# A hybrid RWKV-7, S5 and conv-FFN layer on one core: larger bursts in the level step, GELUs put behind its last copies, squares on GpSimd, and six residuals added through PSUM at the end

## The chip, the cores and the metric

The kernel runs on one core of a Trainium2 chip. The time is device microseconds (us) of one execution of the whole program, from its first to its last instruction and what the runtime puts around it; the table below gives the median of three runs, and one further execution was recorded by the hardware profiler. Engines are named as the profile names them: PE is TensorE (PEld its weight loads), DVE is VectorE, ACT is ScalarE, POOL is GpSimd, SP is SyncE, which here only issues DMAs.

## The reference

One layer over x of 1 x 1024 x 1024 floats (SEQ 1024, D_MODEL 1024), all in float32:

```python
h = rms_norm(x, norm_mix_pre)
proj = h @ w_in                                # [RWKV r,k,v + low-rank downs | S5 input | two gates]
gates = sigmoid(proj[..., N_RWKV_COLS + S5_WIDTH:] + b_gate)
g_rwkv, g_s5 = split(gates, 2)
o_rwkv = rwkv7_branch(proj[..., :N_RWKV_COLS], ...) @ w_branch_rwkv     # 8 heads of 64, delta-rule state
o_s5 = s5_branch(u_s5, ...) @ w_branch_s5      # 32 groups of 16 channels, 64 complex states each:
                                               # y = Re(C s) + D u;  y = gelu(y);  y * sigmoid(y @ w_glu + b_glu)
mixed = (g_rwkv * o_rwkv + g_s5 * o_s5) @ w_out
x = x + rms_norm(mixed, norm_mix_post)
h = rms_norm(x, norm_ffn_pre)
z = causal depthwise conv of width 3 over h @ w_up;  gate, val = split(z)
f = (gelu(gate) * val) @ w_down                # hidden width 2816
x = x + rms_norm(f, norm_ffn_post)
```

## The kernel before

Everything is held transposed: channels on the 128 partitions, time along the free axis in two halves of 512 (called th = 0 and 1). A weight tile is loaded as wf, rounded to fp32r by ACT (wh, L160), and the rest wf - wh is taken by DVE (wl, L161); an activation is split the same way (hh by ACT at L245, hl by DVE at L246). A product of one 128x128 weight block with 512 columns is then three matmuls in a row: wh with hh, wh with hl, wl with hh (L180, L181, L182, one "step"). The order of PE's instructions is written by a small planner in the program: each part of the work is a generator that emits some instructions and yields (its cost on PE, how long its next piece should wait, a weight); lanes of such generators run by priority, and between them `background()` puts in steps from the queue of projections, so that a stated wait of 13 us means 13 us of PE work, by the planner's count, ahead of the next piece. The other four engines' orders come from a list scheduler with priorities; where the program wants a fixed order there it adds one by `add_manual_dep(..., ORDER)`, which sets an order and no semaphore. Each engine takes its instructions in its order; the DMA queues of SP, ACT and POOL are issued in those engines' orders too.

The stages, with the lines the change touches:

- `start` (to about 40 us): the first pre-norm (th = 0), the split of its eight tiles (`self.splits[k]` holds the two instructions, ACT L245 and DVE L246, of tile k), and the S5 input products (PE L1158) with weights loaded by `s5_ws`. `behind_low` is a pair of instructions behind which the following wh and wl casts are ordered.
- S5, four groups b of eight (to about 300 us): tables on DVE, then `s5_batch`: scans (DVE L643), two rotations z*sn and z*cs on DVE (L645, L646), a yield with the stated wait T_SCAN (T_SCAN0 for b = 0), and then 24 matmuls in the order toep, ca, cb (PE L651, L652, L653). L652 reads what L646 wrote.
- RWKV: four blocks i of chunks, each with fronts, a 32x32 triangular inverse on DVE and POOL, `rwkv_level`, and `rwkv_chain` over eight chunks c (PE L870, L888, L899, L901, L906, L911; ACT L874, L903, L909; DVE L902, L913). `rwkv_level` joins 32x32 inverse blocks into 64x64 ones: for each of two steps and each u of two, 16 matmuls of 32x32 into PSUM (L838, then L840), in two halves of 8 with a yield after each half, and two ACT copies out (L839, L841). What L839 writes is what L840 reads.
- The GLU of S5: its inputs come back from DRAM by a POOL DMA (L1253) and go through GELU on ACT (`s5_y`, L1254, the first of them with an ACT_TABLE_LOAD); hh and hl of them feed the GLU's steps. They are ordered behind `self.squared`, an ACT square in an RWKV front (L700).
- Post-norm (to about 895 us): for th = 1 `post_norm` makes eight tiles mx (DVE L1417, L1418), squares each on ACT (L276) and adds the squares up in a chain of seven (DVE L278); PE L264 sums the last one over the partitions, DVE takes the reciprocal root, PE L290 spreads it. Meanwhile the FFN's first up-projections for th = 0 run on PE, ACT moves them out (L1520), and POOL issues their stores to DRAM (L1521, tensors AH).
- FFN up and down to about 1503 us, and the end: for the last half, two sums of squares (sq, DVE L1729) are summed by PE (L264) into ss, DVE makes the root (rv, rsy), PE L290 spreads it to a bank, DVE L1829 scales the eight tiles, and the residual is added in one of two ways: for the tiles 4 to 7 by two matmuls with the identity into one PSUM bank, one with the residual (L1898) and one with the scaled tile (L1831), and an ACT copy out (L1832); for the tiles 0 to 3 by DVE (L1729). SP issues the eight output DMAs (L1835).

Of the kernel before, what the change touches and what calls it, by code (L numbers as in the profile page):

```python
# [14 lines left out]
ALU = mybir.AluOpType  # L15
# [58 lines left out]
class Kern:  # L74
# [195 lines left out]
    def tx(self):  # L270
        return self.nrm.tile([128, 512], F32, tag="Tx", name=self.nm("tx"), bufs=NTX)

    def square_into(self, acc, x):

        sq = self.tm()
        self.nc.scalar.activation(sq, x, AF.Square)  # L276
        if acc is not None:
            self.nc.vector.tensor_tensor(sq, sq, acc, ALU.add)  # L278
        return sq

    def rstd(self, ss, eps, scale):
# [339 lines left out]
    def s5_batch(self, b, d, ys):  # L621

        nc, V, G, A = self.nc, self.nc.vector, self.nc.gpsimd, self.nc.scalar
        s = self.s5
        mm = nc.tensor.matmul
        ca, cb, cs, sn, toep, wT = (d[n] for n in ("ca", "cb", "cs", "sn", "toep", "wT"))

        u8 = self.u8[b]
        z = self.t4(shape=(128, 8, 128))
        G.memset(z[:, :, 0:1], 0.0)  # L630
        rot = self.t4(shape=(128, 8, 128))
        yield 0, T_US
        p1, p2 = (self.chk().rearrange("p (g n) -> p g n", n=128) for _ in range(2))
        for p, o in ((p1, 0), (p2, 1)):
            for g in range(8):
                mm(p[:, g], wT[:, g, o:o + 2, :], u8[:, g, :], start=g % 4 == 0, stop=True, skip_group_check=True)
        r2 = self.t4(shape=(128, 8, 128))
        V.tensor_tensor(rot, p1, cs, ALU.mult)
        V.tensor_tensor(r2, p2, sn, ALU.mult)
        V.tensor_tensor(rot, rot, r2, ALU.add)  # L640
        for g in range(8):
            gg = b * 8 + g
            V.tensor_tensor_scan(z[:, g, 1:128], s["rho"][:, gg:gg + 1].to_broadcast([128, 127]),  # L643
                                 rot[:, g, 0:127], 0.0, ALU.mult, ALU.add)
        V.tensor_tensor(rot, z, sn, ALU.mult)  # L645
        V.tensor_tensor(z, z, cs, ALU.mult)  # L646
        y8 = self.t4(shape=(128, 8, 128))
        yield 3.6, T_SCAN if b else T_SCAN0
        ps = self.chk().rearrange("p (g n) -> p g n", n=128)
        for g in range(8):  # L650
            mm(ps[:, g], toep[:, g], u8[:, g, :], start=g % 4 == 0, stop=False, skip_group_check=True)  # L651
            mm(ps[:, g], ca[:, g, 1:9, :], z[:, g, :], start=False, stop=False, skip_group_check=True)  # L652
            mm(ps[:, g], cb[:, g, 1:9, :], rot[:, g, :], start=False, stop=True, skip_group_check=True)  # L653
        A.copy(y8, ps)
        for th in range(2):
            A.dma_start(ys[th].rearrange("c g j n -> j c g n"), y8[:, :, th * 64:th * 64 + 64])
        yield 5.4, 0
# [166 lines left out]
    def rwkv_level(self, d, spare):  # L824

        A, V = self.nc.scalar, self.nc.vector
        mm = self.nc.tensor.matmul
        gr = d["gr"]
        p0 = self.chk(1).rearrange("p (u c t) -> p u c t", u=2, t=32)
        p0, p1 = [p0[:, u] for u in range(2)], [self.chb().rearrange("p (c t) -> p c t", t=32) for u in range(2)]  # L830
        xz = (self.tg("x", 1, pool=self.rka) if spare else self.tg("ld", NLD)).rearrange("p (u c t) -> p u c t", u=2, t=32)
        top, bot = [[slice(64 * h + o, 64 * h + o + 32) for h in range(2)] for o in (0, 32)]
        t0, t1 = slice(0, 32), slice(32, 64)
        for h, sl in enumerate(top):
            self.levelled = V.transpose(xz[sl].rearrange("p u c t -> p (u c) t"), gr[sl, :, :, h, t0].rearrange("p u c t -> p (u c) t"))
        yield 0, T_LT
        kw = dict(stop=True, skip_group_check=True)
        steps = ((lambda u, c, h: mm(p1[u][bot[h], c], gr[top[h], u, c, h, t1], xz[top[h], u, c], start=c == 0, **kw),  # L838
                  lambda u, h: A.copy(xz[bot[h], u], p1[u][bot[h], 0:8])),  # L839
                 (lambda u, c, h: mm(p0[u][top[h], c], xz[bot[h], u, c], gr[bot[h], u, c, h, t1], start=c == 0, **kw),  # L840
                  lambda u, h: A.copy(gr[top[h], u, :, h, t1], p0[u][top[h], 0:8])))  # L841
        for step, evict in steps:
            for u in range(2):
                for c in range(8):
                    for h in range(2):
                        step(u, c, h)
                    if c % 4 == 3:
                        yield 0.3, 0.3, 2.0
                for h in range(2):
                    evict(u, h)  # L850
            yield 0, T_LV

    def rwkv_chain(self, d):
# [319 lines left out]
    def start(self, xp):  # L1173

        tc = self.tc

        def go(gen, n=1):
            for _ in range(n):
                with tc.high_priority(HPN if gen in norms else HPW):
                    next(gen, None)  # L1180
        with tc.high_priority(HPN):
            xs = [self.load_x(0, xp)]
            self.setup()
            norms = [self.norm(0, xs[0], xp)]
            self.idle = self.gmp()
        consts = self.s5_setup()
        with tc.high_priority(HPS):
            next(consts)
        go(norms[0], 5)
        newton = self.newton  # L1190
        self.behind_x = self.last_x

        def first(o, behind=None):
            with tc.high_priority(HPN - HPW):
                r = []
                for b in (2, 3):
                    self.behind_low = behind
                    r.append(self.load_w(self.a["w_in"][14 + b][:, o:o + 512]))
                return r
        p = first(0, (None, newton))  # L1200
        go(norms[0])
        q = first(512, (self.splits[1][0], self.splits[2][1]))
        self.behind_x, self.behind_low = None, (None, None)
        ws = [[(x[0] + y[0], x[1] + y[1]) for x, y in zip(p, q)]]
        with tc.high_priority(HPW):
            xs.append(self.load_x(1, xp))
            norms.append(self.norm(1, xs[1], xp))
        with tc.high_priority(HP):
            self.nc.sync.dma_start(self.csts[:, 128:NCST], self.a["cst"][:, 128:NCST])
            self.s5w = {}  # L1210
            self.s5_load(0)
            self.s5_load(1)
        a = self.s5_in((2, 3), 0, ws[0])
        go(a, 8)
        with tc.high_priority(HPW):
            ws.append(self.s5_ws((0, 1)))
        with tc.high_priority(HPS):
            self.setup_vecs()
            self.newton = newton
            next(consts, None)  # L1220
        go(a)
        b = self.s5_in((0, 1), 0, ws[1])
        go(b)
        for _ in range(4):
            go(norms[1])
            go(b)
        go(norms[1])
        go(b, 1)
        go(norms[1])
        go(b, 3)  # L1230
        c = self.s5_in((0, 1), 1, ws[1])
        go(c, 9)
        for b in range(2):
            self.load_u8(b)
# [164 lines left out]
    def post_norm(self, src, y, th, gain, resid, store, squares=None):  # L1399


        nc = self.nc
        o = slice(th * 512, th * 512 + 512)
        xs, sq = [], []
# [10 lines left out]
        for k in range(NK):  # L1415
            y = src[k]
            nc.vector.scalar_tensor_tensor(y, y, self.vec(gain, k), bc, ALU.mult, ALU.mult)  # L1417
            (nc.vector if k % 2 or squares is not None else nc.gpsimd).tensor_tensor(y, y, xs[k], ALU.add)  # L1418
            load(k + NTX)
            if squares is not None:  # L1420
                sq.append(self.square_into(sq[-1] if sq else None, y))
                (nc.sync if th else nc.scalar).dma_start(store(k, o), y)
            else:
                (nc.sync if th else nc.gpsimd).dma_start(store(k, o), y)
# [256 lines left out]
    def down(self, dq0, dqf, dqt, dqa, dqs, dqb):  # L1681
# [3 lines left out]
        nc, V, A = self.nc, self.nc.vector, self.nc.scalar  # L1685
# [150 lines left out]
        acc = [None, None]  # L1836
        f = [[None] * NK for _ in range(2)]
        b, x = [bank(m) for m in range(4)], [bank(4 + m) for m in range(4)]
# [47 lines left out]
        d, last = {}, []  # L1886
# [9 lines left out]
        def resid_sum(m, b):  # L1896
            sums[m] = bank(b)
            mm(sums[m], self.cst("ident"), d["xs1"][m], start=True, stop=False)  # L1898
        resid_sum(4, 0)
        resid_sum(5, 1)  # L1900
        self.sumsq(ss, last[0], True)
        self.sumsq(ss, acc[1], False)
        for m, b in ((6, 4), (7, 5)):
            resid_sum(m, b)
        y = self.rstd(ss, 1e-6, 1.0 / D)
        bc = bank(3)
        self.spread(bc, y)
        outputs(1, f[1], bc, d["xs1"], sums)

    def build(self):  # L1910
# [183 lines left out]
                yield from self.urgent(out)  # L2094


T_SCAN0 = 17.0
T_US, T_TAB0, T_TAB, T_TRIG, T_SCAN = 5.0, 26.0, 20.0, 12.0, 13.0
T_LD, T_LT = 14.0, 3.0
NEVA = 4  # L2100
# [92 lines left out]
```

## Time and profile before

| what | value |
|---|---|
| median of 3 runs | 1525.88 us (1525.83 to 1526.22) |
| the profiled execution | 1524.13 us, of which its span is 1522.3 us |
| PE busy | 1469.8 us, 97% of the span |
| DVE busy | 1158.5 us, 76% |
| ACT busy | 726.6 us, 48% |
| POOL busy | 180.2 us, 12% |
| mean granted TensorE clock | 0.991 |

A row of the timeline gives the start, the length in us, the engine, the line, the operation with its output and inputs, how many instructions were put together, and in brackets how long the engine had stood idle before them and whose instruction ended that. A row of the waits gives an engine and line, whom it waited for, and the total, the count and the longest. A table of windows gives the busy time of each engine in each stretch, and PEclk, the mean granted clock there.

### The profile page before, as it was taken

What the parts mean: (1) busy time and instruction counts of PE and PEld (TensorE: products, weight loads), DVE (VectorE), ACT (ScalarE), POOL (GpSimd) and SP (SyncE); (2) the same over time, 40 slices, a digit from 0 to 9 for tenths busy, and PEclk for the clock granted to TensorE, in tenths of its full rate; (3) what the DMA queues carried; (4) which work ended last, traced back from release to release, by engine and by line L of the source; (5) the groups of instructions that cost most, each with busy time, mean ns of one, the idle gap of its engine ahead of it and who ended that gap; (6) DMA issues with size and microseconds to landing.
All of it is one profiled execution on the core that took longest, in us unless ns stands there. A gap on an engine that the chain in (4) does not pass through costs nothing.

```text
span 1522.3 us, 23902 instructions
## 1 busy us (share of the span) xinstructions
PE 1469.8 (97%) x8804; PEld 1166.1 (77%) x8804; DVE 1158.5 (76%) x2157; ACT 726.6 (48%) x1209; POOL 180.2 (12%) x340
## 2 busy tenths in 40 slices
PE   7999999999999998999999999999999999999997
PEld 5788787787677675666788778888888887888875
DVE  7989974765655594975767888888888888698767
ACT  5465444331453434556635555555555555444451
POOL 0022111124021232030110010000000000000000
PEclk9999999999999998999999999999999999999999
DMA  6455344444332446452456575233333336944712
GB/s 211 135 154 159 98 139 145 143 135 152 107 124 96 128 120 192 146 167 70 157 189 199 182 242 180 93 108 117 113 110 117 112 109 225 333 154 138 246 59 111
DMA packets 121558, 225.26 MB, mean 148 GB/s; under 512 B 31024, under 2 KB 37168, under 8 KB 121440
## 3 DMA queue, kind: packets, MB, share of 16 engines
q1 hardware_dynamic: 90576, 154.77, 32.5%
q0 software_dynamic: 21024, 64.71, 12.9%
q10 hardware_dynamic: 9840, 4.24, 1.1%
q8 instruction: 69, 1.13, 0.3%
q14 instruction: 49, 0.40, 0.1%
HBM read 164.16 MB, written 57.41 MB: 146 GB/s over the span
## 4 chain that ended last, share of the span: by engine, by line
PE 44%; DVE 4%; DMA 4%; ACT 1%; issue 1%; SPq 0%; DVEq 0%; ACTq 0%
PE d L1779 8%; PE rp L1600 5%; PE rp L1602 5%; PE rp L1601 5%; PE mm L1602 2%; PE mm L1600 2%; PE mm L1601 2%; DMA st<-in_w_down_dram 2%; PE ch L181 1%; PE mm L180 1%; PE ch L182 1%; PE mm L181 1%; PE gm L180 1%; PE ch L180 1%; PE mm L182 1%
## 5 line engine op out<-in xcount | busy, mean ns | idle before, releaser
L180 PE MATMUL gm<-hh,wh 128*128 128x512 f32 x672 | 283.1, 421 | 1.9 <-DVE ev L1057 1.9
L181 PE MATMUL gm<-hl,wh 128*128 128x512 f32 x672 | 264.9, 394 | 0.1
L182 PE MATMUL gm<-hh,wl 128*128 128x512 f32 x672 | 264.7, 394 | 0.0
L160 ACT CAST wh<-wf 128x512 fp32r<-128x512 f32 x181 | 111.9, 619 | 171.5 <-PE gm L181 88.5
L161 DVE TENSOR_TENSOR wl<-wf,wh 128x512 fp32r<-128x512 f32 x181 | 124.3, 690 | 86.5 <-ACT wh L160 84.5
L180 PEld LDWEIGHTS gm<-hh,wh 128*128 128x128 f32 x672 | 127.0, 189 | 34.3 <-issue 4.0
L182 PEld LDWEIGHTS gm<-hh,wl 128*128 128x128 f32 x672 | 127.0, 189 | 28.1
L181 PEld LDWEIGHTS gm<-hl,wh 128*128 128x128 f32 x672 | 127.4, 190 | 22.5 <-DVE hl L246 1.0
L1779 PE MATMUL d<-xh,wl 128*128 128x512 f32 x308 | 113.5, 392 | 2.1 <-DVE wl L246 2.1
L1779 PE MATMUL d<-xh,wh 128*128 128x512 f32 x308 | 113.9, 393 | 1.1 <-DVE zg L1630 1.1
L1779 PE MATMUL d<-xl,wh 128*128 128x512 f32 x308 | 113.4, 392 | 0.6 <-DVE xl L246 0.6
L1600 PE MATMUL rp<-t,h 128*128 128x512 f32 x252 | 98.3, 390 | 1.4 <-ACT p L1614 1.4
L1602 PE MATMUL rp<-t,l 128*128 128x512 f32 x252 | 98.0, 389 | 0.0
L1601 PE MATMUL rp<-t,h 128*128 128x512 f32 x252 | 98.0, 389 | 0.0
L1779 PEld LDWEIGHTS d<-xh,wl 128*128 128x128 f32 x308 | 58.1, 189 | 15.1 <-DVE wl L246 2.9
L1779 PEld LDWEIGHTS d<-xh,wh 128*128 128x128 f32 x308 | 57.8, 189 | 14.2 <-DVE zg L1630 1.5
L246 DVE TENSOR_TENSOR l<-r,h 128x1024 fp32r<-128x1024 f32 (+1 forms) x40 | 38.9, 971 | 38.9 <-ACT h L245 38.9
L1779 PEld LDWEIGHTS d<-xl,wh 128*128 128x128 f32 x308 | 58.2, 189 | 13.2 <-DVE xl L246 0.9
L245 ACT CAST h<-r 128x1024 fp32r<-128x1024 f32 (+1 forms) x40 | 33.9, 849 | 69.5 <-PE rp L1601 67.2
L1621 DVE SCALAR_TENSOR_TENSOR y<-zv,vecs,y 128x1023 f32<-128x1023 f32 (+1 forms) x42 | 53.7, 1280 | 10.2 <-ACT y L1619 10.2
L1600 PEld LDWEIGHTS rp<-t,h 128*128 128x128 f32 x252 | 47.3, 188 | 11.9 <-ACT p L1614 2.2
L1601 PEld LDWEIGHTS rp<-t,h 128*128 128x128 f32 x252 | 47.3, 188 | 9.8
(476 smaller groups left out, 3338.1 us busy)
## 6 DMA issues: line engine op xcount, KB each, us to landing
r<-in_w_up_dram SPq DMA_DIRECT2D x42, 512.0 KB, 3.5
wf<-in_w_in_dram SPq DMA_DIRECT2D x72, 256.0 KB, 3.1
st<-in_w_down_dram SPq DMA_DIRECT2D x55, 256.0 KB, 4.3
st<-ACT SPq DMA_DIRECT2D x44, 256.0 KB, 4.2
ACT<-y POOLq DMA_DIRECT2D x21, 512.0 KB, 2.9
GT<-ev POOLq DMA_DIRECT2D x32, 256.0 KB, 3.5
wf<-in_w_br_dram SPq DMA_DIRECT2D x32, 256.0 KB, 3.4
wf<-in_w_out_dram SPq DMA_DIRECT2D x32, 256.0 KB, 2.8
```

The lines of the kernel that those rows point to most:

```text
L160: self.last_wh = nc.scalar.copy(h[:, :n], f[:, :n])
L161: low = nc.vector.tensor_tensor(l[:, :n], f[:, :n], h[:, :n].bitcast(F32), ALU.subtract)
L180: mm(ps, a, xh[k], start=a0, stop=False)
L181: mm(ps, a, xl[k], start=False, stop=False)
L182: mm(ps, b, xh[k], start=False, stop=z0)
L245: a = self.nc.scalar.copy(hi, x)
L246: self.split_ops = a, (eng or self.nc.vector).tensor_tensor(lo, x, hi.bitcast(F32), ALU.subtract)
L1600: mm(ps, wh[:, c], xh, start=first and k == 0, stop=False, skip_group_check=True)
L1601: mm(ps, wh[:, c], xl, start=False, stop=False, skip_group_check=True)
L1602: mm(ps, wl[:, c], xh, start=False, stop=k == 3, skip_group_check=True)
L1621: V.scalar_tensor_tensor(y[:, lag:], z[:, 0:1024 - lag], self.vec(nme, i), y[:, lag:], ALU.mult, ALU.add)
L1779: mm(ps, w[:, c], y[:, x], start=start and k == 0, stop=stop and k == 2, skip_group_check=True)
```

## The change

Seven edits. `square_into` takes an engine, and the seven adds of `post_norm` for th = 1 go to GpSimd. The stated waits ahead of the 24 matmuls of the S5 groups become 19, 15.3, 13 and 13 (before: 17, 13, 13, 13). `rwkv_level` emits its 16 matmuls for a u without the yield in the middle, and yields once after them (0.6, 0.3, 1.5) ahead of the copies. The last copy becomes `self.squared`, behind which the GELUs are ordered. In `start`, the casts of the weights of `s5_ws((0, 1))` are ordered behind the split of the pre-norm's last tile. At the end the sum of squares of `last[0]` goes ahead of the first residual, the others change places, and the residuals of tiles 0 and 1 are put through PSUM too, so six of the eight tiles are. Behind the edit to `square_into` the lines of the new kernel have numbers that differ by one or two from those of before.

```diff
--- before.py
+++ after.py
@@ -270,12 +270,12 @@
     def tx(self):
         return self.nrm.tile([128, 512], F32, tag="Tx", name=self.nm("tx"), bufs=NTX)
 
-    def square_into(self, acc, x):
+    def square_into(self, acc, x, eng=None):
 
         sq = self.tm()
         self.nc.scalar.activation(sq, x, AF.Square)
         if acc is not None:
-            self.nc.vector.tensor_tensor(sq, sq, acc, ALU.add)
+            (eng or self.nc.vector).tensor_tensor(sq, sq, acc, ALU.add)
         return sq
 
     def rstd(self, ss, eps, scale):
@@ -645,7 +645,7 @@
         V.tensor_tensor(rot, z, sn, ALU.mult)
         V.tensor_tensor(z, z, cs, ALU.mult)
         y8 = self.t4(shape=(128, 8, 128))
-        yield 3.6, T_SCAN if b else T_SCAN0
+        yield 3.6, T_SCANS[b]
         ps = self.chk().rearrange("p (g n) -> p g n", n=128)
         for g in range(8):
             mm(ps[:, g], toep[:, g], u8[:, g, :], start=g % 4 == 0, stop=False, skip_group_check=True)
@@ -844,10 +844,9 @@
                 for c in range(8):
                     for h in range(2):
                         step(u, c, h)
-                    if c % 4 == 3:
-                        yield 0.3, 0.3, 2.0
+                yield 0.6, 0.3, 1.5
                 for h in range(2):
-                    evict(u, h)
+                    self.squared = evict(u, h)
             yield 0, T_LV
 
     def rwkv_chain(self, d):
@@ -1213,7 +1212,9 @@
         a = self.s5_in((2, 3), 0, ws[0])
         go(a, 8)
         with tc.high_priority(HPW):
+            self.behind_low = self.splits[7]
             ws.append(self.s5_ws((0, 1)))
+            self.behind_low = (None, None)
         with tc.high_priority(HPS):
             self.setup_vecs()
             self.newton = newton
@@ -1418,7 +1419,7 @@
             (nc.vector if k % 2 or squares is not None else nc.gpsimd).tensor_tensor(y, y, xs[k], ALU.add)
             load(k + NTX)
             if squares is not None:
-                sq.append(self.square_into(sq[-1] if sq else None, y))
+                sq.append(self.square_into(sq[-1] if sq else None, y, nc.gpsimd if th else nc.vector))
                 (nc.sync if th else nc.scalar).dma_start(store(k, o), y)
             else:
                 (nc.sync if th else nc.gpsimd).dma_start(store(k, o), y)
@@ -1896,15 +1897,16 @@
         def resid_sum(m, b):
             sums[m] = bank(b)
             mm(sums[m], self.cst("ident"), d["xs1"][m], start=True, stop=False)
+        self.sumsq(ss, last[0], True)
         resid_sum(4, 0)
-        resid_sum(5, 1)
-        self.sumsq(ss, last[0], True)
         self.sumsq(ss, acc[1], False)
-        for m, b in ((6, 4), (7, 5)):
+        for m, b in ((5, 1), (6, 4), (7, 5)):
             resid_sum(m, b)
         y = self.rstd(ss, 1e-6, 1.0 / D)
         bc = bank(3)
         self.spread(bc, y)
+        for m, b in ((0, 6), (1, 7)):
+            resid_sum(m, b)
         outputs(1, f[1], bc, d["xs1"], sums)
 
     def build(self):
@@ -2094,7 +2096,7 @@
                 yield from self.urgent(out)
 
 
-T_SCAN0 = 17.0
+T_SCANS = (19.0, 15.3, 13.0, 13.0)
 T_US, T_TAB0, T_TAB, T_TRIG, T_SCAN = 5.0, 26.0, 20.0, 12.0, 13.0
 T_LD, T_LT = 14.0, 3.0
 NEVA = 4
```

On ACT at the level step of block i = 2, before, the GELUs' table load, three of the first GELUs (L1254) and their splits (hh, L1261) stand ahead of or between the four copies L839 (x from the PSUM banks chb):

```order
L1139 ACTIVATE ev_6167<-gm_6096,hb_b_gate 128x512
L1254 ACT_TABLE_LOAD
L1254 ACTIVATE ev_6274<-ev_6274 128x512
L1254 ACTIVATE ev_6281<-ev_6281 128x512
L1261 CAST hh_6277<-ev_6274 128x512
L160 CAST wh_6566<-wf_6568 128x512
L1261 CAST hh_6284<-ev_6281 128x512
L1254 ACTIVATE ev_6336<-ev_6336 128x512
L839 COPY x_6155<-chb_6154 32x256
L1261 CAST hh_6339<-ev_6336 128x512
L839 COPY x_6155<-chb_6153 32x256
L839 COPY x_6155<-chb_6154 32x256
```

After, the four copies L839 and the four L841 of this level stand with no GELU among them, and the table load comes 14 rows behind the last L841, in the chain, ahead of the copy L902 (UV) of chunk c = 2:

```order
L908 COPY yn_6426<-chk_6516 64x2x64 x2
L895 ACTIVATE spt_6623<-S_2614,pt_4605 128x64 x2
L925 ACTIVATE ar_4784<-yn_6426 128x256
L1255 ACT_TABLE_LOAD
L1255 ACTIVATE ev_6469<-ev_6469 128x512
L160 CAST wh_6804<-wf_6806 128x512
L1262 CAST hh_6472<-ev_6469 128x512
L1255 ACTIVATE ev_6476<-ev_6476 128x512
L1255 ACTIVATE ev_6533<-ev_6533 128x512
L1262 CAST hh_6479<-ev_6476 128x512
L1262 CAST hh_6536<-ev_6533 128x512
L902 COPY UV_5672<-chb_6611 64x128
```

So the table load and three GELUs moved from ahead of the level's copies into the chain. On POOL in the post-norm of th = 1, before, the queue holds only the stores of the FFN's first products:

```order
L1521 DMA AH_149<-t_1788_9421 128x512
L1521 DMA AH_150<-t_1793_9443 128x512
L1521 DMA AH_151<-t_1798_9465 128x512
L1521 DMA AH_152<-t_1803_9487 128x512
L1521 DMA AH_153<-t_1808_9509 128x512
```

After, the chain of adds (L278, tm) stands among them:

```order
L278 TENSOR_TENSOR tm_9334<-tm_9334,tm_9327 128x512
L278 TENSOR_TENSOR tm_9340<-tm_9340,tm_9334 128x512
L278 TENSOR_TENSOR tm_9346<-tm_9346,tm_9340 128x512
L1522 DMA AH_149<-t_1788_9421 128x512
L1522 DMA AH_150<-t_1793_9443 128x512
L278 TENSOR_TENSOR tm_9352<-tm_9352,tm_9346 128x512
L278 TENSOR_TENSOR tm_9358<-tm_9358,tm_9352 128x512
L1522 DMA AH_151<-t_1798_9465 128x512
L278 TENSOR_TENSOR tm_9364<-tm_9364,tm_9358 128x512
L1522 DMA AH_152<-t_1803_9487 128x512
L278 TENSOR_TENSOR tm_9370<-tm_9370,tm_9364 128x512
```

The last add stands behind the store of AH_152. On PE at the end, before (d are PSUM banks, A the residuals, r the scaled tiles 4 to 7, csts the identity):

```order
L1898 MATMUL d_14460<-A_14374,csts 128x512
L1898 MATMUL d_14462<-A_14374,csts 128x512
L264 MATMUL d_14459<-ones_226,sq_14447 128x1 x4
L264 MATMUL d_14459<-ones_226,sq_14457 128x1 x4
L1898 MATMUL d_14472<-A_14377,csts 128x512
L1898 MATMUL d_14474<-A_14377,csts 128x512
L290 MATMUL d_14491<-csts,rsy_14478 128x128 x4
L1831 MATMUL d_14460<-r_2603_13900,csts 128x512
L1831 MATMUL d_14462<-r_2604_13909,csts 128x512
L1831 MATMUL d_14472<-r_2605_13918,csts 128x512
L1831 MATMUL d_14474<-r_2606_13927,csts 128x512
```

After, up to the first of the six scaled tiles:

```order
L264 MATMUL d_14459<-ones_226,sq_14447 128x1 x4
L1899 MATMUL d_14464<-A_14374,csts 128x512
L264 MATMUL d_14459<-ones_226,sq_14457 128x1 x4
L1899 MATMUL d_14470<-A_14374,csts 128x512
L1899 MATMUL d_14472<-A_14377,csts 128x512
L1899 MATMUL d_14474<-A_14377,csts 128x512
L290 MATMUL d_14491<-csts,rsy_14478 128x128 x4
L1899 MATMUL d_14496<-A_14368,csts 128x512
L1899 MATMUL d_14498<-A_14368,csts 128x512
L1832 MATMUL d_14464<-r_2603_13900,csts 128x512
```

The first sum of squares now stands ahead of every residual, one residual stands between the two sums, and two stand between the spreading and the first scaled tile; six L1832 follow. SP issues the last four outputs in the order tile 2, 0, 1, 3 (before 0, 1, 2, 3).

## The prediction

> **What bounds the kernel.** I read the page's busy times first, then the waits of PE, the windows for the granted clock, and the timeline around each long wait.
>
> ```profile
> span 1522.3 us, 23902 instructions
> PE 1469.8 (97%) x8804; PEld 1166.1 (77%) x8804; DVE 1158.5 (76%) x2157; ACT 726.6 (48%) x1209; POOL 180.2 (12%) x340
> ```
>
> PE works 97% of the span, and the edits take no product away. What they can win is idle time of PE (1522.3 - 1469.8 = 52.5 us), matmuls at half clock, and the joints between short and long matmuls.
>
> ```profile
> PE chk L840 <- ACT x L839: 3.8, 2, 3.4
> PE rp L264 <- DVE tm L278: 2.9, 2, 2.1
> PE gm L1158 <- ACT hh L245: 2.7, 3, 1.8
> PE rp L290 <- DVE rsy L143: 1.2, 1, 1.2
> ```
>
> The level, post-norm and start edits aim at these rows. Two windows show what a stop costs behind it:
>
> ```profile
> 575.00:600.00 25.00, 21.11 (x231) 13.59 (x230) 10.93 (x15) 13.09 (x23) 9.94 (x18) 0.80 0.70 216
> 875.00:900.00 25.00, 21.03 (x90) 16.54 (x91) 19.38 (x42) 11.67 (x22) 4.24 (x8) 0.93 0.77 263
> ```
>
> The granted clock (third number from the right) falls to 0.80 behind the 3.4 us stop and to 0.93 behind the 2.1 us stop: (1 - 0.80) x 25 = 5.0 us and (1 - 0.93) x 25 = 1.75 us of full-speed work lost besides the stops.
>
> **The level step and the GELUs.** At i = 2:
>
> ```profile
> 581.66 1.28 ACT L1254 ACT_TABLE_LOAD   x1 [6.03 <-issue]
> 582.96 1.38 ACT L1254 ACTIVATE ev<-ev 128x512 f32<-128x512 f32 x2
> 585.23 0.62 ACT L160 CAST wh<-wf 128x512 fp32r<-128x512 f32 x1
> 587.39 0.36 ACT L839 COPY x<-chb 32x256 f32<-32x256 f32 x1
> 588.86 1.02 ACT L839 COPY x<-chb 32x256 f32<-32x256 f32 x3
> 589.28 0.24 PE L840 MATMUL chk<-gr,x 32*32 32x32 f32 x2 [3.42 <-ACT x L839]
> 589.94 0.63 PE L840 MATMUL chk<-gr,x 32*32 32x32 f32 x14 [0.41 <-ACT x L839]
> ```
>
> ACT stands empty for 6.03 us with the GELU at its head, whose input is still being fetched; the copies L839 queue behind it, and PE stops for 3.42 + 0.41 us. With the clock that is 8.8 us. In the new order the copies have no GELU ahead of them, so these 8.8 us go. What is late next: the table load, three GELUs, a cast and three splits now stand ahead of the copy L902 of chunk c = 2, 1.28 + 3 x 0.69 + 4 x 0.62 = 5.8 us of ACT, behind the squares of chunk 1's moments (about 1.2 us of DVE and ACT work after that chunk's last product). PE has two blocks of six matmuls there, six more and about 0.9 us of chain matmuls, 18 x 0.23 + 0.9 = 5.0 us. The wait is 5.8 + 1.2 - 5.0 = 2.0 us; it is bounded by 0 (the squares run early) and by 5.8 (they run as late as the copy). I take 2.0, plus half a drop of clock like the one at 875, 0.9. Net -8.8 + 2.9 = **-5.9**, between -8.8 and -1.3 (5.8 + 1.75 paid).
>
> [...]
>
> **The bursts.** A half burst in the middle of the long matmuls:
>
> ```profile
> 579.81 0.39 PE L182 MATMUL gm<-hh,wl 128*128 128x512 f32 x1
> 580.13 0.44 PE L838 MATMUL chb<-x,gr 32*32 32x32 f32 x16
> 580.50 0.50 PE L180 MATMUL gm<-hh,wh 128*128 128x512 f32 x1
> 580.84 0.39 PE L181 MATMUL gm<-hl,wh 128*128 128x512 f32 x1
> 581.07 0.40 PE L182 MATMUL gm<-hh,wl 128*128 128x512 f32 x1
> ```
>
> From L182 to the burst 0.32, the burst 0.37, then L180 0.34 against the 0.23 of L181: it costs 0.32 + 0.37 + 0.34 - 2 x 0.23 = 0.57 us, two of them 1.14. One burst of twice the length costs 0.57 + 0.37 = 0.94 at most. That is 0.2 us for each u and step; four blocks have 16 of these, 3.2 us. Some halves already stood next to other short matmuls, where the joint is cheaper, but 0.37 for 16 rows holds a fixed part that a double burst pays once, so the bounds are 0 and 4.8 (0.3 each). Against it: between L838 and L840 there are now 9 to 12 long matmuls, 2.0 to 2.8 us, for two ACT copies of 0.36 that wait their turn on ACT. I take **-2.5**.
>
> **The S5 waits.**
>
> ```profile
> 129.45 0.46 PE L652 MATMUL chk<-t,ca 128*128 128x128 f32 x2 [1.84 <-DVE t L646]
> 165.51 1.22 DVE L646 TENSOR_TENSOR t<-t,t 128x1024 f32<-128x1024 f32 x1
> 166.87 0.77 PE L652 MATMUL chk<-t,ca 128*128 128x128 f32 x2 [2.06 <-DVE t L646]
> 129.00:166.80 37.80, 34.62 (x200) 29.19 (x200) 36.46 (x57) 18.72 (x25) 7.45 (x10) 0.99 0.38 105
> ```
>
> In group 0 the new order puts three steps, 9 x 0.23 = 2.0 us, ahead of the 24 matmuls, which covers the 1.84. In group 1 only two more steps in all (1.4 us) come ahead of them than before. But DVE is the bound here: between the two L646 it has the same instructions in either order and is busy 36.46 of 37.80 us (last row, third busy time), so the second L652 starts when DVE is done at 166.7, whatever PE did meanwhile. Of 1.84 saved, PE then gives back what the second wait grows by. What remains is the work moved ahead of 166.87: two steps, **-1.4**. Bounds: 0, and 1.84 + 2.06 + 1.75 for a drop of clock like the one at 875 = -5.6 if DVE also gains.
>
> **The start.**
>
> ```profile
> 28.06 1.28 ACT L160 CAST wh<-wf 128x512 fp32r<-128x512 f32 x2 [1.88 <-DMA wf<-in_w_in_dram]
> 30.76 1.28 ACT L245 CAST hh<-x 128x512 fp32r<-128x512 f32 x2 [1.42 <-DVE x L1046]
> 31.43 0.74 PE L1158 MATMUL gm<-hh,wh 128*128 128x512 f32 x2 [1.78 <-ACT hh L245]
> ```
>
> The casts stand on ACT waiting 1.88 us for a load, with the split that PE waits for behind them. Turned round, the 1.78 us stop goes; the casts end by about 31, and their first matmuls come at about 32.5. DVE's sums of the next half come a little later for it: **-1.3**, between 0 and -1.8.
>
> **Squares on GpSimd.** No two-input GpSimd operation is in this trace. The rows near it:
>
> ```profile
> 110.30 0.80 POOL L1094 TENSOR_SCALAR ev<-ev 128x512 f32<-128x512 f32 x1
> 110.55 1.09 DVE L161 TENSOR_TENSOR wl<-wf,wh 128x512 fp32r<-128x512 f32 x1
> 155.36 2.66 POOL L1074 TENSOR_SCALAR ev<-ev 128x512 f32<-128x512 f32 x1 [3.48 <-ACT ev L1073]
> 878.10 0.54 POOL L1521 DMA_DIRECT2D AH<-t  x1 [2.04 <-ACT t L1520]
> 883.71 0.69 DVE L278 TENSOR_TENSOR tm<-tm,tm 128x512 f32<-128x512 f32 x1
> 884.45 1.05 PE L264 MATMUL rp<-ones,tm 128*128 128x1 f32 x8 [2.05 <-DVE tm L278]
> ```
>
> Before, the seventh add ends at 884.4 and PE waits from 882.4. Seven adds of 0.69 leave DVE (4.8 us), so the last tile mx comes about 5 us earlier, at 877 instead of 882.2 or so. The last add stands behind the store of 878.10, out at 878.6. An add takes between 0.69 (DVE's) and 2.66 (the longest GpSimd row); I take 1.4, twice DVE's and nearer the row of 0.80. The last then ends at 880, or 881.3 at the long price: ahead of PE either way, if the chain keeps up (six adds over the 14 us from 862 to 876 need 2.3 or less each). The stop (2.05) and its clock (1.75) go, 3.8; some of it may come back at L290, whose wait of 1.2 hangs on DVE: **-3.0**, bounds -5.0 (with L290's) and the loss worked out under the rivals.
>
> **The end.**
>
> ```profile
> 1505.36 1.84 PE L264 MATMUL d<-ones,sq 128*128 128x1 f32 x16
> 1507.06 1.96 PE L1898 MATMUL d<-A,csts 128*128 128x512 f32 x4
> 1509.62 1.16 PE L290 MATMUL d<-csts,rsy 128*128 128x128 f32 x8 [0.60 <-DVE rsy L143]
> 1511.62 3.70 PE L1831 MATMUL d<-r,csts 128*128 128x512 f32 x8 [0.84 <-DVE r L1829]
> 1515.36 0.58 ACT L1832 COPY r<-d 128x512 f32<-128x512 f32 x1 [0.27 <-PE d L1831]
> 1517.30 1.29 DVE L1729 TENSOR_TENSOR q<-q,A 128x512 f32<-128x512 f32 x2
> ```
>
> L264 starts at 1505.36, when the squares are there, in either order; before, two residuals stood ahead of it and filled the wait. One sum takes 0.85 (1507.06 - 1505.36 for both), one bank 0.86 (the ACT copies come 0.58 + 0.27 apart). After: sum, residual, sum end at 1507.9 instead of 1507.06, so the root and L290 come 0.85 later, at 1510.5; two residuals behind L290 (1.0) put the first L1831 at 1513.2. The fourth copy starts 3.74 behind the first L1831 (1515.36 - 1511.62), the sixth 1.7 later, and it takes 0.58: 1519.2. DVE's last add ends at 1518.6 before, and at 1511.65 + 8 x 0.69 + 1.29 = 1518.5 after. The last output goes out at 1519.3 instead of 1518.6: **+0.7**, between -0.9 (DVE two adds, 1.3 us, shorter, and the extra residuals in idle slots) and +1.6 (the first scaled tile's delay in full).
>
> **Sum.** -5.9 - 2.5 - 1.4 - 1.3 - 3.0 + 0.7 = -13.4. The profiled execution, 1524.13, would be 1510.7; the median of runs stands 1.75 higher, so 1512.5. Moves of a row or two that this does not price (level and chain of i = 3, the projection steps that slide as the planner's counts change) are worth up to 2 either way; waits come easier than they go, and I say 1513.0.
>
> **Rivals.** (a) Waits only move. ACT and DVE, not PE's order, set the S5, level and chain times: bursts and scans bring 0, the GELU term its poor end -1.3, start -1.3, norm -3.0, end +0.7: -4.9, 1521.0. For it speaks that DVE is 76% busy and saturated in S5; against it, that ACT is 48% busy and stood empty for 6 us just there.
> (b) No change to be told: (a), and the GpSimd adds are as late as DVE's were, 0 for the norm: -1.9, 1524.0.
> (c) Slower, by the adds on GpSimd alone.
>
> ```profile
> 862.00:884.50 22.50, 19.04 (x83) 14.79 (x81) 18.06 (x31) 12.41 (x22) 2.71 (x5) 1.00 0.87 281
> ```
>
> The row of 110.55 shows a DVE subtraction of two inputs taking 1.09 beside a GpSimd operation on SBUF, not 0.69. If every add holds DVE for its whole length, seven of 2.66 take 18.6 us of DVE in place of 4.8, and the row of the window gives DVE 22.50 - 18.06 = 4.4 us idle: 18.6 - 4.8 - 4.4 = 9.4 us late, with the weight splits (wl) of the FFN behind it, and the clock's 5.0 us as behind the longest stop above. Against the other terms' -10.4 that is +4.0, 1529.9. It decides from 2.1 us an add on (7 x 2.1 = 4.8 + 4.4 - 5.0 + 10.4). Against it: the delay seen was 0.4 and the GpSimd row beside it took 0.80, not 2.66.
> [...]
> (d) Everything comes full: start -1.8, scans -5.6, bursts -4.8, GELU -8.8, norm -5.0, end -0.9 is 1499; half of what that adds to my sum gives 1506.
>
> **Chances.** The forecast, 1507 to 1519.5 as the single terms miss by their halves: 0.62; (a) 0.18; (b) 0.08; (c) 0.05; (d) 0.07. A measurement here tells 0.2% (3.05 us) from no change: below 1522.8 is faster, to 1528.9 the same. Of (a), 0.03 falls in the same band, and the moderate half of (c). Faster 0.62 + 0.15 + 0.07 = 0.84, shaded to 0.82; same 0.13; slower 0.05. Leaving out (c), half of (b) and the far half of (d), the range is 1506 to 1523.
>
> **What will show it.** Right: no L840 <- ACT x L839 above 0.5, the table load behind L925, a wait of PE in the chain of i = 2 at L905 or L181 of 1 to 3 us; no L1158 wait at 31; the first L652 wait near 0 and the second near 3; POOL L278 rows of 0.8 to 2 us and L264's wait gone; first L1831 (then L1832) 1.6 later after the last product, the end 0.7 later. Wrong: a clock still below 0.9 in 575 to 600, POOL rows above 2.4 with DVE rows stretched beside them, or an L840 wait at the other three levels.

## The result, and the profile after

The changed kernel takes 1538.3 us (median of six runs, 1535.55 to 1545.16) against 1525.86 of before (six runs too): a ratio of 1.0109, interval 1.0085 to 1.0133. It is 1.1% slower; 1513.0 was predicted. The profiled execution is 1536.52 with a span of 1534.4. The first rows of its page:

```profile
span 1534.4 us, 23915 instructions
PE 1472.4 (96%) x8812; PEld 1170.6 (76%) x8812; DVE 1158.9 (76%) x2148; ACT 727.9 (47%) x1211; POOL 187.7 (12%) x347
```

PE's waits that are new, or gone, from the table of its waits:

```profile
PE gm L180 <- ACT hh L250: 6.1, 1, 6.1
PE chk L900 <- ACT p L873: 5.8, 2, 5.5
PE chb L838 <- DVE x L835: 4.9, 2, 4.2
PE chb L898 <- DVE p L890: 4.2, 2, 3.0
PE gm L180 <- ACT ev L1091: 3.7, 1, 3.7
PE chk L652 <- DVE t L646: 0.3, 1, 0.3
PE rp L264 <- DVE tm L278: 0.2, 1, 0.2
```

The waits that the edits aimed at are small now: L652, L264, and L840 and L1158 (now L1157) are below 1 us. Five others of 3 to 6 us stand there instead (the first five rows), and four of the five lie between 500 and 710 us. The windows show what that stretch costs; the first row is of the kernel before, the second of the changed one, then 710 to 1500 in the same order (columns: the window and its length, busy time and instructions of PE, PEld, DVE, ACT and POOL, then PEclk, DMA share, GB/s):

```profile
500.00:710.00 210.00, 198.00 (x1842) 144.26 (x1831) 146.70 (x395) 109.75 (x245) 45.82 (x84) 0.98 0.48 143
```
```profile
500.00:710.00 210.00, 182.70 (x1644) 135.29 (x1642) 140.72 (x377) 101.77 (x223) 43.29 (x80) 0.93 0.46 136
```
```profile
710.00:1500.00 790.00, 777.38 (x3595) 636.21 (x3594) 635.50 (x861) 394.20 (x564) 43.03 (x80) 1.00 0.48 157
```
```profile
710.00:1500.00 790.00, 781.60 (x3632) 638.32 (x3631) 633.07 (x852) 399.09 (x574) 52.71 (x87) 1.00 0.48 157
```

Count as lost the time in which PE is idle, and the share of the window that the clock lacks. From 500 to 710 that was 12.0 + 0.02 x 210 = 16 us and is 27.3 + 0.07 x 210 = 42 us. From 710 to 1500 it was 12.6 and is 8.4, the post-norm among it. So the loss sits in this stretch, which holds the end of the chain of block 1 (the stop at L898, at 508), the level and chain of block 2 (L838 at 570, L900 at 605) and the GLU (L180 at 653). It is some 26 us by this rough count: the clock has two digits, so each sum is good to about 1 us, and half clock inside a stop is counted twice. Part of it is won back elsewhere: the span grew by 12.1. (Joints between short and long matmuls count as busy and do not show in these sums: before, L180 behind the burst at 580.13 took 0.34 us to the next start, the L181 after it 0.23.)

### The profile page after: what moved, and what is told of

It reads as the page before. It is cut to its first block, busy times and chain, and to the rows that moved or that the text cites. A ratio compares the mean times of both kernels' runs of the same rounds, so it can differ in the third digit from the quotient of the medians.

```text
span 1534.4 us, 23915 instructions
## 1 busy us (share of the span) xinstructions
PE 1472.4 (96%) x8812; PEld 1170.6 (76%) x8812; DVE 1158.9 (76%) x2148; ACT 727.9 (47%) x1211; POOL 187.7 (12%) x347
## 4 chain that ended last, share of the span: by engine, by line
PE 73%; DVE 12%; DMA 6%; issue 3%; ACT 3%; SPq 1%; POOL 1%; ACTq 0%; DVEq 0%; POOLq 0%
PE d L1780 10%; PE gm L180 9%; PE gm L181 8%; PE gm L182 8%; PE rp L1603 5%; PE rp L1601 5%; PE rp L1602 5%; PE mm L1602 2%; PE mm L1601 2%; PE mm L1603 2%; DVE wl L161 2%; DMA wf<-in_w_up_dram 1%; PE ch L181 1%; PE mm L180 1%; PE mm L181 1%
## 5 line engine op out<-in xcount | busy, mean ns | idle before, releaser
L180 PE MATMUL gm<-hh,wh 128*128 128x512 f32 x672 | 283.9, 422 | 8.5 <-ACT hh L250 6.1
L181 PE MATMUL gm<-hl,wh 128*128 128x512 f32 x672 | 266.3, 396 | 0.1
L180 PEld LDWEIGHTS gm<-hh,wh 128*128 128x128 f32 x672 | 127.9, 190 | 41.7 <-ACT hh L250 6.5
L181 PEld LDWEIGHTS gm<-hl,wh 128*128 128x128 f32 x672 | 128.4, 191 | 23.3 <-DVE hl L246 1.0
```

Source lines behind the costliest of these rows:

```text
L180: mm(ps, a, xh[k], start=a0, stop=False)
L181: mm(ps, a, xl[k], start=False, stop=False)
```

## The experiments

Each was compared with runs of the kernel before on the same chip. Times of one kernel mostly spread by about 0.5% to either side (for instance, 35 runs of the kernel before: 1517.09 to 1529.90, median 1522.30), so the ratios with their 95% intervals are what counts.

**One edit each, and the GELU order taken out.** The first leaves the changed kernel as it is but for this:

```diff
-                    self.squared = evict(u, h)
+                    evict(u, h)
```

> The changed kernel without one line: the GELUs are not ordered behind the level's last copy. Theory A (the order of the GELUs puts the table load, three GELUs and their splits of 1 us each into the chain of block 2, and with it late GLU inputs later on): the 5.5 us stop at the chain (L900 waiting for ACT p) and the 6.1 us stop (L180 waiting for ACT hh L250) go with their half clock, about 12 + 7 us, so 1517 to 1523. Rival B (larger bursts and shorter level steps bring the level and the chain ahead of what DVE, POOL and the DMAs can deliver; the GELUs' order hardly matters): above 1531, with stops of several us at L838, the chain or the GLU still there.

Measured: 1.0084 (1.0054 to 1.0114), against 1.0109 (1.0085 to 1.0133) with the line. Theory A falls: its trace has the same two stops, 5.5 us at L900 and 6.2 at L180.

The line alone, on the kernel before:

```diff
-                    evict(u, h)
+                    self.squared = evict(u, h)
```

> The kernel before with the one line alone: PE's order is that of before, on ACT the first two copies L839 come ahead of the table load. A: the stop of 3.4 us at L840 shrinks but the GELUs come no earlier for it; slower than before by 3 or more, above 1529. B: 3 to 8 us faster, 1518 to 1523, as the stop and its half clock go and nothing else moves.

Measured: 1.0041 (1.0021 to 1.0060), slower, as A had it for this run and not B. Its longest stop at L840 is 3.1 us, for a copy L841 in place of L839.

The bursts alone:

```diff
-                    if c % 4 == 3:
-                        yield 0.3, 0.3, 2.0
+                yield 0.6, 0.3, 1.5
                 for h in range(2):
                     evict(u, h)
```

> The kernel before with the larger bursts alone. A: 0 to 5 us faster (the joints), 1521 to 1526. B: slower, 1530 or more, with new stops between 500 and 710 us that before did not have.

Measured: 1.0116 (1.0088 to 1.0145). This one edit has the whole loss. From its waits, the same stops as in the changed kernel:

```profile
PE gm L180 <- ACT hh L250: 6.3, 1, 6.3
PE chk L900 <- ACT p L873: 6.1, 2, 5.8
PE chb L838 <- DVE x L835: 4.7, 2, 4.0
PE chb L898 <- DVE p L890: 4.0, 2, 2.8
```

The GELUs are not ordered behind anything new here, and yet the table load stands in the chain.

The adds on GpSimd alone (the two edits in `square_into` and `post_norm`):

> The kernel before with the seven adds of the post-norm on GpSimd alone. If the trace of the changed kernel is read rightly there (no stop at L264): 3 to 5 us faster, 1521 to 1523. If the adds hold DVE back or the clock is lowered by a stop a little later: within 1.5 us of before. Adds of about 1.4 us on POOL in either case.

Measured: 0.9974 (0.9956 to 0.9993), faster by 4 us. The seven adds on POOL, in the table of groups:

```profile
L278 POOL TENSOR_TENSOR tm<-tm,tm 128x512 f32<-128x512 f32 x7 | 9.6, 1366 | 90.4 <-ACT tm L276 89.9 <-issue 0.4
```

**The bursts, or the yields?** The edit to the level does two things: it joins two half bursts, and it yields once with 0.6 x 1.5 where it yielded twice with 0.3 x 2.0. The planner puts in other work for each yield: in PE's order before, 27 long matmuls stand within each level, after, 12 to 18. Ahead of the first chain step of block 2 that counts 1707 before and 1674 after, 33 fewer, 7.5 us at 0.227 each. The same matmuls come later, behind the chains. So the next run joins the bursts and keeps the yields:

```diff
-                    if c % 4 == 3:
-                        yield 0.3, 0.3, 2.0
+                yield 0.3, 0.3, 2.0
+                yield 0.3, 0.3, 2.0
                 for h in range(2):
                     evict(u, h)
```

> The kernel before with full bursts of 16, but with both yields of before (0.3, 0.3, 2.0) kept, one behind the other, after them: the bursts are merged, and the planner puts as much other work into the level as before (1707 long matmuls stand ahead of the first chain step of block 2, as before; in the changed kernel 1674). Theory C (what costs is that the level takes less other work with it, so the RWKV path runs ahead of its fillers and of DVE and POOL): 1 to 5 us faster than before, no stop above 2 us at L838 or in the chain of block 2. Theory D (the merged bursts themselves cost): slower by 8 or more.

Measured: 0.9983 (0.9966 to 1.0001). Joined bursts by themselves don't cost anything that can be told; 1.3% lies between the two forms of yield. In the changed kernel, the same:

```diff
-                yield 0.6, 0.3, 1.5
+                yield 0.3, 0.3, 2.0
+                yield 0.3, 0.3, 2.0
```

> The changed kernel with one line different: after a full burst the two yields of before (0.3, 0.3, 2.0 twice) in place of one of 0.6, 0.3, 1.5, so 1707 long matmuls stand ahead of the first chain step of block 2, not 1674. Theory C (the fillers): 16 us or more come back; 1518 to 1523 beside 1522 for before (singles: bursts with fillers -0.17%, squares -0.26%, scans -0.18%, start -0.12%, end +0.20%, GELU order up to +0.4%). Theory A' (the GELU order costs by itself, 0.4% as it did alone): 1525 to 1529. Above 1533: C is wrong.

Measured: 1.0010 (0.9988 to 1.0032) in place of 1.0109. One line takes back 0.99%. From 500 to 710 this kernel loses 210 - 191.73 + 0.02 x 210 = 22 us, not 42:

```profile
500.00:710.00 210.00, 191.73 (x1774) 141.54 (x1773) 147.11 (x396) 109.28 (x246) 45.20 (x83) 0.98 0.48 142
```

Does it matter where that other work stands? With the changed bursts and yields, and more of it drawn behind the copies:

```diff
-T_KN, T_BK, T_GR, T_INV, T_LV, T_CH, T_LN, T_LF = 12.0, 10.0, 2.5, 58.0, 1.0, 0.8, 12.0, 12.0
+T_KN, T_BK, T_GR, T_INV, T_LV, T_CH, T_LN, T_LF = 12.0, 10.0, 2.5, 58.0, 3.2, 0.8, 12.0, 12.0
```

> The kernel before with the changed kernel's bursts and yields, and the stated wait behind each half of the level 3.2 in place of 1.0: the other work that the burst's yield no longer draws is drawn behind the copies; 1710 long matmuls ahead of the first chain step of block 2. Theory C: what counts is how much other work stands ahead of the chain, not where in the level; so within 4 us of before, 1518 to 1526. If it has to stand between a burst and its copies: 1530 or more.

Measured: 1.0042 (1.0021 to 1.0062). Between the two: more than half of the loss is taken back, not all, so theory C in its plain form, by the count ahead of the chain alone, falls short. Its waits show the stop ahead of level 2 still there. PE comes to that level at 577.7, later than before (576.1), but the transposes that make the level's input (L835) end at 582.7 instead of 573.9, after a wait of POOL of 4.3 us for the DMAs that store the inverse; what exactly sets them back was not tried:

```profile
PE chb L838 <- DVE x L835: 4.7, 2, 4.3
```

Which levels? Joined bursts everywhere, with the changed yield only in some blocks (the others keep both yields):

```diff
-                    if c % 4 == 3:
-                        yield 0.3, 0.3, 2.0
+                if self.nat < 2:
+                    yield 0.6, 0.3, 1.5
+                else:
+                    yield 0.3, 0.3, 2.0
+                    yield 0.3, 0.3, 2.0
```

> The kernel before with full bursts in all four blocks, the changed yield (0.6, 0.3, 1.5) in blocks 0 and 1 only, both yields of before in blocks 2 and 3. Long matmuls ahead of the level of block 2: 1635, as in the changed kernel (before 1659). If the lead that the first two levels give is what costs (the RWKV path ahead of POOL, the DMAs and DVE): 1531 or more, with stops at L838 of block 2 and at the chain. If the missing fillers of levels 2 and 3 cost: within 4 us of before.

Measured: 1.0072 (1.0050 to 1.0094). The reverse (`self.nat >= 2`):

> The reverse: the changed yield in blocks 2 and 3 only; 1659 long matmuls ahead of the level of block 2, as before, and 6 fewer through it. If the lead of the first levels is what costs: within 4 us of before, 1519 to 1527. If the fillers in levels 2 and 3: 1531 or more.

Measured: 1.0013 (0.9998 to 1.0028). The fillers missing from levels 0 and 1 are the larger part. They are paid for later: these two rows are of the first of the two runs, whose longest stop at L902 is in the chain of block 1 (at 513 us), with one of 2.2 in that of block 2, and whose stop at L838 is ahead of level 2:

```profile
PE chb L902 <- DVE p L894: 5.3, 3, 2.7
PE chb L838 <- DVE x L835: 4.8, 2, 4.0
```

**The other edits.** The S5 waits alone (`T_SCANS`):

> The kernel before with the stated waits 19, 15.3, 13, 13 alone. In the changed kernel's trace both L652 stops went, but L180 stopped 3.7 us for ACT (ev, L1091) between them, with half clock behind it. If that stop belongs to the waits: 0 to 2 us slower or faster. If it came from another edit: 3 to 5 us faster.

Measured: 0.9982 (0.9964 to 1.0000); its trace has the stop of 3.7 us at L180 too, so that stop belongs to the stated waits.

The end alone:

> The kernel before with the new end alone. By the sum in the prediction 0.7 us slower; in the changed kernel's trace the end from the last product to the last matmul grew by about 4 us, 1.7 of it half clock. Expected 0.5 to 4 us slower, and the six copies 0.86 us apart behind one another.

Measured: 1.0020 (1.0000 to 1.0040), 3 us slower, by an interval that just reaches zero.

The start alone:

> The kernel before with the casts of the first weights of S5 groups 0 and 1 ordered behind the norm's last split, alone. The 1.8 us stop at L1158 goes and PE's order stays: 1 to 2 us faster. If DVE, which bounds the S5 stage, sets the end of it, 0.

Measured: 0.9988 (0.9971 to 1.0005): in the direction expected, and within what can't be told from nothing.

**Together.** Squares, scans and start:

> The kernel before with the three edits that were not slower alone (squares on GpSimd, the S5 waits, the start), nothing else. If they add up: -0.26 - 0.18 - 0.12 = -0.56%, 8.5 us, about 1514. If two of them win the same time: -0.3%.

Measured: 0.9984 (0.9965 to 1.0003), a gain of 0.16% where the three singles add up to 0.56%. The sum has an interval of its own, about 0.25 to 0.87% from those of the singles, so that they overlap is likely and not certain; which two would is open. With joined bursts and both yields:

> The same three and the merged bursts with both yields kept. If it all adds up: -0.73%, 1511 to 1512. If the merged bursts gain nothing beside the others: as the run with the three.

Measured: 0.9971 (0.9951 to 0.9992). It beats both kernels: 0.3% below before, 1.4% below the changed one.

**The GELUs behind the level, with the fillers kept.** The planner emits the first GELUs within level 2, so in the kernel before the ordering line could reach only the copies already emitted. This run moves them two gates later as well, on the run with squares, scans and start:

```diff
-                    evict(u, h)
+                    self.squared = evict(u, h)
...
-MGAP = 3
-XS0 = {1: (0, 1), 2: (2, 3)}
+MGAP = 5
+XS0 = {3: (0, 1), 4: (2, 3)}
```

> The run with squares, scans and start, and the GELUs truly put behind the level's last copy with the fillers as before: the ordering line, and the merge takes its first GELUs two gates later (emitted behind the level, their GLU tiles two gates later too). All copies L839 and L841 of block 2 then stand ahead of the table load. If the GELU term of the prediction was right in kind: the stop of 3 us at L840 and its half clock go, 5 to 8 us less than the run with the three (1519): 1511 to 1514. If the cluster only moves its stop into the chain: 1518 to 1523.

Measured: 1.0025 (1.0010 to 1.0039), against 0.9984 without: 0.4% slower, and above both of the ranges expected. The stop at L840 went, and these two came:

```profile
PE chk L888 <- ACT p L874: 7.5, 4, 4.6
PE gm L180 <- ACT hh L250: 4.7, 1, 4.7
```

With joined bursts and both yields besides:

> The same with the merged bursts and both yields kept: 1 to 3 us less than without them if the joints count, the same if not.

Measured: 0.9975 (0.9955 to 0.9995), 0.5% below the run without the joined bursts, more than expected; why was not tried. Against 0.9971 for the run without the GELU edits, the GELUs' place made no difference there that can be told.

## Why the prediction was wrong

**The bursts: the step that failed.** The prediction priced what a burst costs between two long matmuls and took the rest as cover ("there are now 9 to 12 long matmuls ... for two ACT copies"). The term was put at -2.5 us, between 0 and -4.8, and the edit alone measured +1.16%, some 18 us. The joints themselves were sized about right. In the run with joined bursts and both yields, one whole burst and the matmuls beside it are:

```profile
457.64 0.39 PE L182 MATMUL gm<-hh,wl 128*128 128x512 f32 x1
457.95 0.69 PE L838 MATMUL chb<-x,gr 32*32 32x32 f32 x32
458.58 0.50 PE L180 MATMUL gm<-hh,wh 128*128 128x512 f32 x1
458.92 0.40 PE L181 MATMUL gm<-hl,wh 128*128 128x512 f32 x1
```

Counted as in the prediction it costs 0.31 + 0.63 + 0.34 - 2 x 0.23 = 0.82 us, against 1.14 for two halves: 0.3 saved, for 0.2 forecast. That run measured -0.17%, 2.6 us, with an interval from 5.2 us less to nothing. What was left out is that a yield is also a purchase of other work. The changed one buys less, and "Moves of a row or two that this does not price", put at "up to 2 either way", measured +20 us (1.0116 against 0.9983 of 1522). 33 fewer long matmuls stand ahead of the chain of block 2; the RWKV path came that much earlier on PE, and then met work that does not run on PE. At level 2 of the changed kernel, first on PE, then on DVE and POOL:

```profile
573.91 0.24 PE L838 MATMUL chb<-x,gr 32*32 32x32 f32 x2 [4.24 <-DVE x L835]
```
```profile
573.16 0.70 DVE L835 STREAM_TRANSPOSE x<-gr 32x512 f32<-32x512 f32 x1 [3.07 <-DMA gr<-xd]
```
```profile
567.39 4.59 POOL L822 DMA_DIRECT2D gr<-xd  x8 [1.24 <-DMA xd<-x]
```

The level's transposes wait for eight DMAs that bring the inverse back from DRAM (gr<-xd), which POOL issues one by one in 4.59 us, and these wait for the DMAs that store it there (xd<-x). Before, in the same order:

```profile
576.10 0.44 PE L838 MATMUL chb<-x,gr 32*32 32x32 f32 x16
```
```profile
573.16 0.70 DVE L835 STREAM_TRANSPOSE x<-gr 32x512 f32<-32x512 f32 x1
```
```profile
565.79 4.64 POOL L822 DMA_DIRECT2D gr<-xd  x8 [1.09 <-DMA xd<-x]
```

The eight DMAs took as long before (4.64 us), and the last transpose ended at 573.9, against 574.7 in the changed kernel. So the level's input comes no earlier, while PE, with 24 fewer long matmuls ahead of the level, is there at 569.7 instead of 576.1. The lead was lost on DVE, in the 31 steps of the triangular inverse: their adds (L812) begin 5.2 us earlier, at 522.4 instead of 527.6, and end no earlier. The windows from the first to the last, before and then changed, show DVE (third busy time) nearly full in both, with 6.3 us more work beside them in the second:

```profile
527.60:559.40 31.80, 30.48 (x165) 25.45 (x164) 29.74 (x119) 14.91 (x29) 4.11 (x9) 1.00 0.34 106
```
```profile
522.40:560.05 37.65, 37.09 (x213) 30.49 (x212) 36.09 (x123) 14.31 (x26) 5.39 (x10) 1.00 0.33 106
```

In the chain of block 1, DVE of the changed kernel stood with a scan (L718) at its head that waited 4.51 us for a DMA, and the add that PE waited for (L890) behind it:

```profile
510.12 1.23 DVE L718 TENSOR_TENSOR_SCAN ld<-csts,ld 128x512 f32<-128x512 f32 x1 [4.51 <-DMA ld<-TZ]
511.27 0.26 DVE L890 TENSOR_TENSOR p<-p,chk 128x128 f32<-128x128 f32 x1
```

**The GELUs: no gain in any run, for a reason of its own.** The prediction paid 2.0 us and half a drop of clock in the chain for 8.8 taken away. In the changed kernel, on ACT:

```profile
603.64 1.28 ACT L1255 ACT_TABLE_LOAD   x1
604.93 0.63 ACT L1255 ACTIVATE ev<-ev 128x512 f32<-128x512 f32 x1
605.47 0.60 ACT L160 CAST wh<-wf 128x512 fp32r<-128x512 f32 x1
605.98 1.07 ACT L1262 CAST hh<-ev 128x512 fp32r<-128x512 f32 x1
606.95 1.16 ACT L1255 ACTIVATE ev<-ev 128x512 f32<-128x512 f32 x2
608.00 2.03 ACT L1262 CAST hh<-ev 128x512 fp32r<-128x512 f32 x2
610.05 0.26 ACT L902 COPY UV<-chb 64x128 f32<-64x128 f32 x1
610.32 0.27 ACT L873 COPY p<-chk 128x128 f32<-128x128 f32 x1
656.16 0.63 ACT L1255 ACTIVATE ev<-ev 128x512 f32<-128x512 f32 x1 [3.40 <-DMA ev<-YU]
```

The place was foreseen (in the chain, behind L925), the size not. A split of a GELU (L1262) takes 1.06 to 1.10 us, not the 0.62 of a weight cast that was used (1.09 stood in the trace of before as well, and was read past); the cluster is 6.4 us, not 5.8. The prediction also let PE work on through 18 long matmuls; in fact PE came to the copies 1.5 us after the cluster began, and stopped for 5.48 us, for L900 waits for the copy p (L873), which stands behind the cluster as L902 does. The GLU's inputs come late too, and its product waits 6.11 us for them (hh, L250); the GELU of the last of them waits for its DMA until 656.16, and how much of this the cluster causes is not shown. With the fillers and the half bursts as before, in the run with the ratio 1.0025, the two stops are 4.6 and 4.7, and that run is 0.4% slower than the one without the GELU edits (0.9984). So ordering the GELUs behind the copies moves the stop of 3.4 us, and a second one at the GLU comes with it. With joined bursts and both yields the two can't be told apart (0.9975 and 0.9971). Why the kernel before is better off with its GELUs in the level is shown only this far: there the GLU's inputs are ready when wanted. In the changed kernel the line itself decides little, since with the bursts alone the table load stands in the chain anyway.

The prediction allowed for half a drop of the clock behind a stop of 2.0 us. The stop was 5.48 us, so it does not tell whether one of 2.0 would have cost clock; the last section has rows on that. The stop of 5.48 did bring half clock, in the window around its end:

```profile
609.00:615.00 6.00, 4.36 (x30) 3.21 (x30) 5.66 (x15) 3.42 (x7) 0.62 (x2) 0.50 0.38 108
```

The window from 500 to 710 lacks 0.07 x 210 = 15 us of clock in all.

**The squares: right.** -3.0 was forecast, 4 us were measured (1 to 7). An add took 1.37 us (1.4 taken). L264's wait, 2.9 us before, was 0.2 in the changed kernel and 0.9 with this edit alone, where L290's rose from 1.2 to 1.8, as the prediction allowed. DVE did feel it, as rival (c) had it, but not for long enough:

```profile
877.23 1.29 POOL L278 TENSOR_TENSOR tm<-tm,tm 128x512 f32<-128x512 f32 x1 [84.37 <-DMA tx<-in_x_dram]
877.34 2.33 DVE L1419 TENSOR_TENSOR mx<-mx,tx 128x512 f32<-128x512 f32 x2
881.89 1.78 DVE L1419 TENSOR_TENSOR mx<-mx,tx 128x512 f32<-128x512 f32 x1
```

DVE's adds of 0.69 take up to 1.78 beside them: they end 1.1 us later, nearly a whole GpSimd add. DVE's idle time took that up: in the 22.5 us up to L264 it was busy 18.06 before (862 to 884.5) and 21.96 in the changed kernel (871.8 to 894.3).

**The S5 waits: the size by luck (2.7 us measured, 0 to 5.5, for 1.4 forecast), wrong in working.** The second L652 stop did not grow; it went too, since another wait took its place ahead of it: L180 for a low-rank activation on ACT behind a table load, 3.7 us at 140. The two L652 stops and one at L651 had been 4.4, so the stops explain 0.7 us of the gain at most; where the rest comes from is open.

**The start: in the direction forecast, and not more.** 1.3 us were forecast and 1.8 measured, with an interval that reaches zero. The stop of 1.78 at L1158 is gone in the trace, but it was a large one to begin with: in the traces of nine other kernels without this edit the longest stop there is 0.6 to 1.0 us. The term was taken from one execution.

**The end: the mechanism right, the size not.** Alone it costs 3 us (0 to 6) for +0.7. In the trace of that run the first scaled tile's matmul comes 9.3 us after the last product, not 7.8: 1.5 later, where 1.6 was forecast. The span ends 1.4 later, twice the forecast and inside its bounds. In the changed kernel the wait for the squares, 1.38 us that PE now spends idle, was followed by half clock as well (0.50 from 1517 to 1520):

```profile
1514.22 1.05 PE L264 MATMUL d<-ones,sq 128*128 128x1 f32 x8 [1.38 <-DVE sq L1730]
1517.02 4.38 PE L1899 MATMUL d<-A,csts 128*128 128x512 f32 x6
```

The six matmuls took 4.38 us there. In the run with the end alone the same wait of 1.38 us brought no half clock (1.00 from 1504 to 1515), and they took 2.82:

```profile
1509.81 2.82 PE L1898 MATMUL d<-A,csts 128*128 128x512 f32 x6
```

**The rivals.** None had this mechanism. (a) came nearest in kind, with waits that only move, but ended at 1521, because it set the bursts' poor end at 0 where they measured +1.16%. (c) put the loss on the adds, which were a gain.

## What to carry to other kernels

In a kernel whose order is bought by stated costs and weights, an edit to a yield moves work for hundreds of microseconds behind it: count the fillers ahead of each serial step in both orders before pricing the edit itself, and where the count changes, put the fillers back first and measure the edit alone. A serial path that gets ahead of its fillers gains nothing if its next step hangs on another engine's queue; here it came 6.4 us sooner to level 2, waited 4.2 us there, and half clock followed (0.50 from 576 to 581). A group of instructions that stands in the way on one engine has to go somewhere: price it at its new place with the durations of its own rows.

## What the runs showed of the hardware

The same stop was followed by a lowered clock in one execution and not in another. Here are the windows around L180's wait of 1.9 us at 250, in the kernel before and in the run with the end alone, whose instructions are the same up to there (the wait is 1.87 us in both):

```profile
245.00:260.00 15.00, 13.13 (x58) 10.56 (x57) 5.53 (x10) 7.35 (x12) 2.87 (x11) 1.00 0.81 252
```
```profile
245.00:260.00 15.00, 13.13 (x51) 10.36 (x50) 5.03 (x9) 7.64 (x12) 2.88 (x11) 0.89 0.72 220
```

PE is busy 13.13 us in both, but at a clock of 1.00 and of 0.89, so 1.65 us less work was done. What decides between the two was not shown. With half a dozen stops of about 2 us in the kernel (six of 1.8 to 2.1 among its waits), at some 1.7 us each (1.65 here, 1.75 behind the stop of 2.05 at L264), this could spread its time by several microseconds (an estimate from these numbers) without any edit, and a price "for the clock" behind a stop of 2 us is a chance, not a sum.
